# Another order for the first weights and tokens, and the adding transfers behind the first tile of the first closing

## The chip, the cores and the metric

One core of one Trainium2 chip runs the whole kernel in one launch. The metric is the device time of one execution in microseconds, as a median over runs; lower is better. A verdict compares the changed kernel with the kernel before on the same chip.

## The reference

The kernel is a two-layer decoder trunk on 512 tokens of width 1024 in float32. The first layer mixes with a gated short convolution, the second with sliding-window attention over a shared K and V; both are followed by a SwiGLU network of width 2816. Cut to the parts that the change touches:

```
def short_conv_mixer(h, w_in, conv_w, w_out):
    bcx = h @ w_in
    b_gate, c_gate, u = jnp.split(bcx, 3, axis=-1)
    y = b_gate * causal_depthwise_conv3(c_gate * u, conv_w)
    return y @ w_out

mix = short_conv_mixer(rmsnorm(h, a_pre_norm[l]), a_w_in[l], a_conv_w[l], a_w_out[l])
h = h + rmsnorm(mix, a_post_norm[l])
...
ff = swiglu(rmsnorm(h, ffn_pre_norm[l]), ffn_w_gate_up[l], ffn_w_down[l])
h = h + rmsnorm(ff, ffn_post_norm[l])
```

## The kernel before

Every float32 product is made as three faster products. A matrix is split into a high part (ScalarE rounds it, `AF.Copy` into fp32r) and a low part (VectorE subtracts the high part from the original). TensorE then adds high by high, high by low and low by high. The helper `mm3` holds these three at lines L191, L192 and L193, so nearly all products of the kernel carry one of these lines.

**The start.** The 1024 input features lie in eight token parts `xt[k]` of 128 features by 512 tokens. The first output group of the convolution needs three tiles of `w_in` (for the c, u and b gates, `first[0..2]`, 128 x 1024 each, one block of 128 columns for each `k`). For `k` from 0 to 7 there are nine products of 128 x 512 into three banks `begun[0]` (named `pcub` in the profile): three passes for each of the three tiles, 72 in all, at L687. What they read is made by `token_hi` (L675, ScalarE), `token_lo` (L678, VectorE), `first_hi` (L667, ScalarE) and `first_lo` (L671, VectorE). Ahead of them TensorE runs `WARM` products of ones by ones into an unused bank (`idle`, L663); each of them shows as two in the profile.

The inputs come by transfers that the queue of SyncE (SP) and that of ScalarE (ACT) issue. Each of the three tiles is cut by column into pieces of 256, 256 and 512 columns (`CUTS`, `piece`, L220), so that the first block of all three tiles needs three pieces. The transfers of these two queues share eight semaphores in turn, and the ninth waits until the first has landed, the tenth until the second, and so on. All instructions of TensorE, VectorE, ScalarE and GpSimd stand in the order in which they are written (`manual_schedule`), and each engine works its own list in that order.

**The adding transfers.** Some weight blocks are used as sums of blocks. The sums are made in HBM by transfers that GpSimd issues: `Sums` holds their steps (copy a block, then add another onto it), `sum_on(name)` moves all begun sums on by one step, and `issue(n)` writes the next n transfers into GpSimd's list (L535). An adding transfer waits in that list until the copy under it has landed. Such a step stands at many named places of the kernel (`BEGIN` says which sums begin where).

**The closing.** `close` multiplies the gated convolution by the second half of `w_out`, for four tiles `t` of 128 tokens and two halves of 512 columns each (`unit`, bank `pmix`, 12 products of 128 x 512 for a half), and ends the layer: `take` (L259, VectorE) adds the bank to `mix`; `square_mix` (L264, ScalarE) sums the squares; `tile_done` then scales `mix` (L290), has GpSimd take the power -1/2 of the mean (`mean`, L293 on VectorE and L297 on GpSimd), updates the residual `hs[t]` (`update`, L302, VectorE), squares it (L310), takes a second power of GpSimd for the tile before (`mean2`, L315 and L319) and writes the normalised `xn[t-1]` (`norm`, L324, ScalarE). In the last half of the last tile TensorE transposes `xn[0]` and `xn[1]` (`turn`, L335) between its products. The first closing stands at about 159 to 185 us of the profile; right ahead of it the lines

```
    with tc.manual_schedule(engines=ALL):
        sum_on("o1")
        issue(len(issues))
        close(ws, ys, 0, res, ahead)
```

put the step `o1` into GpSimd's list before any of the closing's powers: two adding transfers onto gate sums begun at `o0`, and four copies that begin the sums `d01`.

Of the kernel before, what the change touches and what calls it, by code (L numbers as in the profile page):

```python
# [10 lines left out]
F32 = mybir.dt.float32  # L11
F32R = mybir.dt.float32r
AF = mybir.ActivationFunctionType
ALU = mybir.AluOpType
PSUM = bass.MemoryType.PSUM

P = 128
D = 1024
S = 512
KT = D // P  # L20
# [18 lines left out]
)  # L39

LAST = (9, 7, 5, 3)
WARM = 10
LEAD = 2
LINE_LEAD = 3

# [27 lines left out]
def yoco_kernel(  # L73
# [139 lines left out]
    xt = [halves("xt") for _ in range(KT // 2)]  # L213
    xt = [xt[k // 2][k % 2] for k in range(KT)]
    first = [wraw.tile([P, D], F32, tag="raw", name=name("raw")) for _ in range(3)]
    CUTS = [(0, 2), (2, 4), (4, KT)]

    def piece(queue, t, c):
        c = slice(CUTS[c][0] * P, CUTS[c][1] * P)
        queue.dma_start(first[t][:, c], w_in[0, t, :, c])  # L220

    nc.scalar.dma_start(gt, gains)
    nc.sync.dma_start(xt[0], xT[0])
    piece(nc.scalar, 0, 0)
    piece(nc.sync, 2, 0)
    piece(nc.scalar, 1, 0)
    nc.sync.dma_start(xt[1], xT[1])
    for t in range(3):
        piece(nc.sync, t, 1)
    nc.sync.dma_start(xt[2], xT[2])  # L230
    nc.sync.dma_start(xt[3], xT[3])
    for t in range(3):
        piece(nc.sync, t, 2)
    for k in range(4, KT):
        nc.sync.dma_start(xt[k], xT[k])
    later = [fetch(w_in[1, t]) for t in range(min(3, N_RAW - 3))]


# [316 lines left out]
    def sum_on(at):  # L555

        issue(len(issues))
        if at in BEGIN:
            summing.append(sums_of[BEGIN[at]])
        for x in summing:  # L560
            x.step()
        summing[:] = [x for x in summing if x.steps]
# [94 lines left out]
    with tc.manual_schedule(engines=ALL):  # L657

        warm = small.tile([P, 1], F32, tag="warm", name=name("warm"))
        nc.scalar.activation(warm, ones[:, 0:1], AF.Copy)  # L660
        idle = bank("idle", ps_pt)
        for _ in range(WARM):
            nc.tensor.matmul(idle[:, :P], ones, ones, start=True, stop=True)  # L663

        def first_hi(t, k0, k1):
            c = slice(k0 * P, k1 * P)
            nc.scalar.activation(ws[t][0][:, c], first[t][:, c], AF.Copy)  # L667

        def first_lo(t, k0, k1):
            c = slice(k0 * P, k1 * P)  # L670
            nc.vector.tensor_tensor(out=ws[t][1][:, c], in0=first[t][:, c],  # L671
                                    in1=ws[t][0][:, c].bitcast(F32), op=ALU.subtract)

        def token_hi(k):
            nc.scalar.activation(xs[k][0], xt[k], AF.Copy, scale=g(G_APRE, k))  # L675

        def token_lo(k):
            nc.vector.scalar_tensor_tensor(  # L678
                out=xs[k][1], in0=xt[k], scalar=g(G_APRE, k), in1=xs[k][0].bitcast(F32),
                op0=ALU.mult, op1=ALU.subtract,  # L680
            )

        def products(k, passes):
            kk = slice(k * P, (k + 1) * P)
            for i, t in passes:
                whi, wlo = ws[t]
                nc.tensor.matmul(begun[0][t], (whi, whi, wlo)[i][:, kk],  # L687
                                 xs[k][i == 1], start=k == i == 0,
                                 stop=k == KT - 1 and i == 2)

        token_hi(0)
        for t in range(3):
            first_hi(t, 0, 1)
        first_lo(0, 0, 1)
        first_lo(1, 0, 1)
        token_lo(0)
        first_lo(2, 0, 1)
        for t in range(3):
            first_hi(t, 1, 2)
        products(0, [(0, 0), (0, 1), (0, 2), (2, 0), (2, 1), (1, 0), (1, 1), (1, 2), (2, 2)])  # L700
        for k in range(1, KT):
            token_hi(k)
            token_lo(k)
            for k0, k1 in CUTS:
                if k == max(k0 - 1, 1):
                    for t in range(3):
                        if k0:
                            first_hi(t, k0, k1)
                    for t in range(3):
                        first_lo(t, max(k0, 1), k1)  # L710
            products(k, [(i, t) for i in range(3) for t in range(3)])
        later += [fetch(w_in[1, t]) for t in range(len(later), 3)]
        for b in range(NB):
            hs[b] = wide("h")
            nc.sync.dma_start(hs[b], x[b])
        nc.sync.dma_start(mask, tables[:, 2 * S :])
        nc.sync.dma_start(snk, sinks.partition_broadcast(P))
        ws = [split_weights(None, raw, True) for raw in later[:2]]
        square(0)
        square(1)  # L720
        ws.append(split_weights(None, later[2], True))
        square(2)
# [136 lines left out]
    def tile_done(res, t, square=True):  # L859

        if t > 0:
            res.mean2(t - 1)
        res.scale(t, 0)
        res.mean(t)
        if t > 0:
            res.norm(t - 1)
        res.scale(t, 1)
        res.update(t)
        if square:
            res.square(t)  # L870

    def close(ws, x, k0, res, ahead):


        n = len(x) - k0

        def part(ps, t, half, ks):
            unit(ps, t, ws[len(ws) // 2 * half :], x, ks, n, k0)

        begun = [bank("pmix", ps_mm) for _ in range(2)]  # L880
        for half in range(2):
            part(begun[half], 0, half, range(n - 1))
            ahead.one()
            ahead.one()
        for t in range(NB):
            for half in range(2):
                if t == 0:
                    ps = begun[half]
                    part(ps, t, half, range(n - 1, n))
                else:  # L890
                    ps = bank("pmix", ps_mm)
                    if (t, half) == (NB - 1, 1):
                        part(ps, t, half, range(2))
                        for b in range(4):
                            res.turn(b, (0, 1))
                        part(ps, t, half, range(2, n))
                        for f in range(4):
                            res.split(0, f, 0)
                        res.square_mix(t, 0)
                        res.square(NB - 2)  # L900
                        res.scale(t, 0)
                    else:
                        part(ps, t, half, range(n))
                res.take(t, half, ps)
                if (t, half) != (NB - 1, 0):
                    res.square_mix(t, half)
            if t < NB - 1:
                tile_done(res, t, square=t < NB - 2)

    def last_tile(res, pieces, ahead=None):  # L910

# [42 lines left out]
    issue(len(issues))  # L954
    ahead = Ahead(first_weights(0))
    with tc.manual_schedule(engines=ALL):
        sum_on("o1")
        issue(len(issues))
        close(ws, ys, 0, res, ahead)


    def ffn(l, before, ahead, gain, gpres, following):
# [539 lines left out]
def _lay_out(x, a_pre_norm, a_w_in, a_conv_w, a_w_out, a_post_norm, ffn_pre_norm,  # L1502
# [7 lines left out]
    def stationary(w, n):  # L1510

        w = np.asarray(w)
        k = w.shape[0] // P
        return w.reshape(k, P, n, P).transpose(2, 1, 0, 3).reshape(n, P, k * P)
# [27 lines left out]
    for b in (0, HD):  # L1542
# [6 lines left out]
    tables[:, 2 * S :] = np.where((diff >= 0) & (diff < P), 0.0, -1e30)  # L1549

    wi = stationary(a_w_in[0], 3 * KT).reshape(3, KT, P, D)
    gu = np.stack([stationary(ffn_w_gate_up[l], 2 * NF).reshape(2, NF, P, D) for l in range(2)])
    gu = gu.transpose(0, 2, 1, 3, 4)
    gb = gu[:, PLAIN:].reshape(2, -1, 2, 2, P, 2, S).transpose(0, 1, 3, 5, 4, 2, 6)
# [6 lines left out]
        "behind": c(behind),  # L1561
        "sinks": c(np.asarray(b_sinks)[0][heads]),
        "tables": tables,
        "w_in": c(wi[[1, 2, 0]].transpose(1, 0, 2, 3)),
        "w_ob": c(blocks(np.asarray(a_w_out[0])[: D // 2])),
        "w_out": c(moving(np.asarray(a_w_out[0])[D // 2 :])),
        "w_gu": c(gu[:, :PLAIN]),
# [24 lines left out]
```

## Time and profile before

| | us |
|---|---|
| median of 3 runs | 1030.83 (1030.18 to 1030.97) |
| the profiled execution's own time | 1033.09 |
| its span, first to last instruction | 1031.3 |
| TensorE busy in it | 1019.1 (99%) |

The profiled execution took 2.26 us more than the median, and 1.79 us of its own time lie outside the span. In the rows of the timeline the first two numbers are the start and the duration in us; then follow the engine, the line, the operation, what is written and read, and how many are merged. The bracket at the end of a row gives the idle time of that engine ahead of it and what ended the idle time. SPq, ACTq and POOLq are the sequencers of these engines, which issue transfers; PEld is TensorE's weight load. A product's duration reaches past the start of the next, so the distance from start to start tells its cost.

### The profile page before, as it was taken

To read this page: it belongs to the slowest core of one execution; us is meant where nothing else is said; L and a number is where in the kernel's file an instruction comes from. 1 tells how busy PE (TensorE), PEld (TensorE's weight loads), DVE (VectorE), ACT (ScalarE), POOL (GpSimd) and SP (SyncE) were. 2 spreads that over 40 slices of the span, in tenths; PEclk is the share of its full clock that TensorE was granted. 3 is DMA by queue.
4 is the path that set the end of the run, shared out by engine and by line. 5 is a ranking of instruction groups with operands and counts; after the bars stand their busy time and mean duration, and the time that the engine had idled before them with its cause. 6 is when DMAs were issued, how large, how long until landed. Compare 5 with 4: busy or idle time off the path is not lost.

```text
span 1031.3 us, 17485 instructions
## 1 busy us (share of the span) xinstructions
PE 1019.1 (99%) x6650; PEld 927.5 (90%) x6650; DVE 822.4 (80%) x1404; ACT 577.6 (56%) x1039; POOL 193.9 (19%) x259
## 2 busy tenths in 40 slices
PE   9999999999999999999999999999999999999997
PEld 7888887999989899999898888889998999989986
DVE  5676666888777978878869998688886788887786
ACT  7232543865655454566466777668565554645632
POOL 0433122102101021000122663221211010200001
PEclk9999999999999999999999999999999999999999
DMA  9897789548979789868603879986889676998732
GB/s 332 288 247 232 192 251 338 167 164 253 330 237 275 262 281 301 280 209 308 194 1 128 219 206 274 256 268 164 257 283 326 184 248 201 315 299 248 246 139 82
DMA packets 66868, 244.59 MB, mean 237 GB/s; under 512 B 7904, under 2 KB 8800, under 8 KB 55008
## 3 DMA queue, kind: packets, MB, share of 16 engines
q1 hardware_dynamic: 51472, 145.91, 38.7%
q0 software_dynamic: 14592, 96.48, 36.6%
q8 instruction: 52, 0.85, 0.3%
q10 hardware_dynamic: 720, 1.08, 0.3%
q14 instruction: 32, 0.26, 0.1%
HBM read 237.15 MB, written 102.76 MB: 330 GB/s over the span
## 4 chain that ended last, share of the span: by engine, by line
PE 89%; DVE 4%; DMA 4%; ACT 1%; POOL 1%; issue 1%; ACTq 0%; DVEq 0%; POOLq 0%
PE gx L193 7%; PE gx L192 7%; PE gx L191 7%; PE gz L193 4%; PE gz L192 4%; PE gz L191 4%; PE px L191 3%; PE px L192 3%; PE px L193 3%; PE pcub L192 3%; PE pcub L193 3%; PE pcub L191 3%; DMA hsum<-in_w_gb_dram 3%; PE pmix L193 2%; PE pmix L192 2%; PE pmix L191 2%
## 5 line engine op out<-in xcount | busy, mean ns | idle before, releaser
L467 DVE TENSOR_TENSOR wlo<-raw,whi 128x1024 fp32r<-128x1024 f32 x225 | 275.1, 1227 | 94.0 <-ACT whi L466 93.9
L466 ACT ACTIVATE whi<-raw 128x1024 fp32r<-128x1024 f32 x225 | 234.3, 1050 | 120.1 <-DVE raw L454 22.0
L191 PE MATMUL gx<-xt,whi 128*128 128x256 f32 x480 | 135.8, 283 | 0.0
L192 PE MATMUL gx<-xt,whi 128*128 128x256 f32 x480 | 135.8, 283 | 0.0
L193 PE MATMUL gx<-xt,wlo 128*128 128x256 f32 x480 | 135.8, 283 | 0.0
L535 POOL DMA_DIRECT2D hsum<-in_w_gb_dram x96 | 62.9, 720 | 159.1 <-ACT whi L466 82.3
L191 PEld LDWEIGHTS gx<-xt,whi 128*128 128x128 f32 x480 | 92.2, 192 | 0.0
L192 PEld LDWEIGHTS gx<-xt,whi 128*128 128x128 f32 x480 | 92.2, 192 | 0.0
L193 PEld LDWEIGHTS gx<-xt,wlo 128*128 128x128 f32 x480 | 92.2, 192 | 0.0
L1011 ACT ACTIVATE st<-gx 128x256 f32<-128x256 f32 x80 | 30.3, 385 | 80.8 <-PE gx L193 80.8
L535 POOL DMA_DIRECT2D hsum<-hsum x32 | 25.2, 789 | 262.9 <-ACT whi L466 186.6
L192 PE MATMUL pcub<-xhi,whi 128*128 128x512 f32 x168 | 65.4, 389 | 0.0
L191 PE MATMUL pcub<-xlo,whi 128*128 128x512 f32 x168 | 65.4, 389 | 0.0
L193 PE MATMUL pcub<-xhi,wlo 128*128 128x512 f32 x168 | 65.4, 389 | 0.0
L191 PE MATMUL px<-wlo,ahi 128*128 128x512 f32 x120 | 46.7, 389 | 0.0
L193 PE MATMUL px<-whi,alo 128*128 128x512 f32 x120 | 46.7, 389 | 0.0
L192 PE MATMUL px<-whi,ahi 128*128 128x512 f32 x120 | 46.7, 389 | 0.0
L193 PE MATMUL gx<-xhi,wlo 128*128 128x256 f32 x160 | 45.3, 283 | 0.0
L191 PE MATMUL gy<-xlo,whi 128*128 128x256 f32 x160 | 45.3, 283 | 0.0
L192 PE MATMUL gy<-xhi,whi 128*128 128x256 f32 x160 | 45.3, 283 | 0.0
L193 PE MATMUL gy<-xhi,wlo 128*128 128x256 f32 x160 | 45.3, 283 | 0.0
L191 PE MATMUL gz<-xt,whi 128*128 128x256 f32 x160 | 45.3, 283 | 0.0
(268 smaller groups left out, 3120.3 us busy)
## 6 DMA issues: line engine op xcount, KB each, us to landing
hsum<-in_w_gb_dram POOLq DMA_DIRECT2D x96, 512.0 KB, 8.1
raw<-hsum SPq DMA_DIRECT2D x88, 512.0 KB, 7.8
raw<-in_w_gb_dram SPq DMA_DIRECT2D x60, 512.0 KB, 7.4
hsum<-in_w_dn_dram POOLq DMA_DIRECT2D x36, 512.0 KB, 8.3
raw<-in_w_dn_dram SPq DMA_DIRECT2D x32, 512.0 KB, 6.6
hsum<-hsum POOLq DMA_DIRECT2D x28, 512.0 KB, 5.4
raw<-in_w_in_dram SPq DMA_DIRECT2D x21, 512.0 KB, 7.8
hsum<-in_w_dn_dram POOLq DMA_DIRECT2D x12, 768.0 KB, 13.2
```

Of the source, the lines that this page charges most:

```text
L191: nc.tensor.matmul(out, whi, xlo, start=start, stop=False, **kw)
L192: nc.tensor.matmul(out, whi, xhi, start=False, stop=False, **kw)
L193: nc.tensor.matmul(out, wlo, xhi, start=False, stop=stop, **kw)
L466: self.begun = nc.scalar.activation(hi[:, :n], raw, AF.Copy)
L467: nc.vector.tensor_tensor(out=lo[:, :n], in0=raw, in1=hi[:, :n].bitcast(F32), op=ALU.subtract)
L535: nc.gpsimd.dma_start(dst, src, max_dma_last_dim=4 * 4 * S, **kw))
L1011: nc.scalar.activation(s, x, AF.Copy)
```

## The change

Three things are edited; the arithmetic of the sums stays as it was but for the order of the passes.

First, the 24 blocks (128 columns each) of the first three tiles are laid out on the host in the order in which the products use them: for `k` = 0 the blocks of the three gates, then those for `k` = 1, and so on. `first[0]` holds blocks 0 to 7, `first[1]` 8 to 15, `first[2]` 16 to 23. The pieces are now runs of this order: 384, 384 and 256 columns of the first, and halves of 512 columns of the other two. All that `k` = 0 needs of the weights is one piece, issued by SP behind `xt[0]`; the second piece is the only one on ScalarE's queue. Pieces and token parts follow each other on SP's queue in the order of use.

Second, the splitting follows the same order (the table `FIRST`), the nine products for each `k` run as high by high, low weight by high token, high weight by low token, and `WARM` is 9 instead of 10.

Third, the step `o1` of the adding transfers is handed to `close` as `then` and stands in GpSimd's list behind the first tile's power instead of ahead of it.

```
-WARM = 10
+WARM = 9
...
-    CUTS = [(0, 2), (2, 4), (4, KT)]
-    def piece(queue, t, c):
-        c = slice(CUTS[c][0] * P, CUTS[c][1] * P)
-        queue.dma_start(first[t][:, c], w_in[0, t, :, c])
+    def piece(queue, i, c0, c1):
+        queue.dma_start(first[i][:, c0:c1], w_in[0, i, :, c0:c1])
     nc.scalar.dma_start(gt, gains)
     nc.sync.dma_start(xt[0], xT[0])
-    piece(nc.scalar, 0, 0)
-    piece(nc.sync, 2, 0)
-    piece(nc.scalar, 1, 0)
+    piece(nc.sync, 0, 0, 384)
+    piece(nc.scalar, 0, 384, 768)
     nc.sync.dma_start(xt[1], xT[1])
-    for t in range(3):
-        piece(nc.sync, t, 1)
     nc.sync.dma_start(xt[2], xT[2])
+    piece(nc.sync, 0, 768, D)
+    piece(nc.sync, 1, 0, S)
     nc.sync.dma_start(xt[3], xT[3])
-    for t in range(3):
-        piece(nc.sync, t, 2)
-    for k in range(4, KT):
-        nc.sync.dma_start(xt[k], xT[k])
+    piece(nc.sync, 1, S, D)
+    nc.sync.dma_start(xt[4], xT[4])
+    piece(nc.sync, 2, 0, S)
+    nc.sync.dma_start(xt[5], xT[5])
+    piece(nc.sync, 2, S, D)
+    nc.sync.dma_start(xt[6], xT[6])
+    nc.sync.dma_start(xt[7], xT[7])
...
-        token_hi(0)
-        for t in range(3):
-            first_hi(t, 0, 1)
-        first_lo(0, 0, 1)
-        first_lo(1, 0, 1)
-        token_lo(0)
-        first_lo(2, 0, 1)
-        for t in range(3):
-            first_hi(t, 1, 2)
-        products(0, [(0, 0), (0, 1), (0, 2), (2, 0), (2, 1), (1, 0), (1, 1), (1, 2), (2, 2)])
-        for k in range(1, KT):
+        FIRST = {0: [(0, 0, P), (0, P, 384)], 1: [(0, 384, 768)], 2: [(0, 768, D), (1, 0, S)],
+                 4: [(1, S, D)], 5: [(2, 0, S)], 6: [(2, S, D)]}
+        for k in range(KT):
+            pieces = FIRST.get(k, [])
             token_hi(k)
+            for p in pieces:
+                first_hi(*p)
+            for p in pieces:
+                first_lo(*p)
             token_lo(k)
-            for k0, k1 in CUTS:
...
-            products(k, [(i, t) for i in range(3) for t in range(3)])
+            for i in range(3):
+                for t in range(3):
+                    n = 3 * k + t
+                    whi, wlo = (w[:, n % KT * P : (n % KT + 1) * P] for w in ws[n // KT])
+                    nc.tensor.matmul(begun[0][t], (whi, wlo, whi)[i], xs[k][i == 2],
+                                     start=k == i == 0, stop=k == KT - 1 and i == 2)
...
-    def close(ws, x, k0, res, ahead):
+    def close(ws, x, k0, res, ahead, then=None):
...
             if t < NB - 1:
                 tile_done(res, t, square=t < NB - 2)
+            if t == 0 and then:
+                then()
...
     with tc.manual_schedule(engines=ALL):
-        sum_on("o1")
-        issue(len(issues))
-        close(ws, ys, 0, res, ahead)
+        def sums_on():
+            sum_on("o1")
+            issue(len(issues))
+        close(ws, ys, 0, res, ahead, sums_on)
...
     wi = stationary(a_w_in[0], 3 * KT).reshape(3, KT, P, D)
+    wi = c(wi[[1, 2, 0]].transpose(1, 0, 2, 3))
+    wi[0] = wi[0].reshape(3, P, KT, P).transpose(2, 0, 1, 3).reshape(3, KT, P, P).transpose(
+        0, 2, 1, 3).reshape(3, P, D)
...
-        "w_in": c(wi[[1, 2, 0]].transpose(1, 0, 2, 3)),
+        "w_in": wi,
```

More of the change, by code (lines that the diff above doesn't have):

```diff
@@ L663, in yoco_kernel, with first_hi, first_lo @@
             nc.tensor.matmul(idle[:, :P], ones, ones, start=True, stop=True)
[L665 to L672, printed above, removed]
+        def first_hi(i, c0, c1):
+            nc.scalar.activation(ws[i][0][:, c0:c1], first[i][:, c0:c1], AF.Copy)
+        def first_lo(i, c0, c1):
+            nc.vector.tensor_tensor(out=ws[i][1][:, c0:c1], in0=first[i][:, c0:c1],
+                                    in1=ws[i][0][:, c0:c1].bitcast(F32), op=ALU.subtract)
         def token_hi(k):
@@ L681, in token_lo @@
             )
[L683 to L689, printed above, removed]
-        token_hi(0)
-        for t in range(3):
-            first_hi(t, 0, 1)
-        first_lo(0, 0, 1)
-        first_lo(1, 0, 1)
-        token_lo(0)
-        first_lo(2, 0, 1)
-        for t in range(3):
-            first_hi(t, 1, 2)
-        products(0, [(0, 0), (0, 1), (0, 2), (2, 0), (2, 1), (1, 0), (1, 1), (1, 2), (2, 2)])
-        for k in range(1, KT):
+        FIRST = {0: [(0, 0, P), (0, P, 384)], 1: [(0, 384, 768)], 2: [(0, 768, D), (1, 0, S)],
+                 4: [(1, S, D)], 5: [(2, 0, S)], 6: [(2, S, D)]}
+        for k in range(KT):
+            pieces = FIRST.get(k, [])
             token_hi(k)
+            for p in pieces:
+                first_hi(*p)
+            for p in pieces:
+                first_lo(*p)
             token_lo(k)
-            for k0, k1 in CUTS:
[L705 to L710, printed above, removed]
-            products(k, [(i, t) for i in range(3) for t in range(3)])
+            for i in range(3):
[4 more added lines that the diff above has]
+                                     start=k == i == 0, stop=k == KT - 1 and i == 2)
         later += [fetch(w_in[1, t]) for t in range(len(later), 3)]
```

## The prediction

> **What bounds the kernel now.** I read the head of the page first, then TensorE's waits, then the timeline where those waits lie.
>
> ```profile
> span 1031.3 us, 17485 instructions
> PE 1019.1 (99%) x6650; PEld 927.5 (90%) x6650; DVE 822.4 (80%) x1404; ACT 577.6 (56%) x1039; POOL 193.9 (19%) x259
> ```
>
> TensorE is busy for 99% of the span. No product is taken out, so the change can only gain where TensorE stands idle or slow, and can lose wherever it makes TensorE wait. The waits of TensorE name few such places:
>
> ```profile
> PE xt L335 <- ACT xn L324: 2.5, 1, 2.5
> PE idle L663 <- DVE ones L140: 1.1, 1, 1.1
> PE pcub L687 <- ACT whi L667: 1.0, 1, 1.0
> ```
>
> Two of the three are in the stages that the change edits: the first products (`pcub`, L687) and the transposes of the first closing (`xt`, L335). Both are waits for something upstream, so I look at each in the timeline. First TensorE at the start:
>
> ```profile
> 1.06 4.64 PE L663 MATMUL idle<-ones 128*128 128x128 f32 x20 [1.06 <-DVE ones L140]
> 5.35 0.77 PE L687 MATMUL pcub<-xhi,whi 128*128 128x512 f32 x1
> 7.13 1.22 PE L687 MATMUL pcub<-xhi,whi 128*128 128x512 f32 x2 [1.00 <-ACT whi L667]
> ...
> 9.00 1.48 PE L687 MATMUL pcub<-xlo,whi 128*128 128x512 f32 x3
> 10.28 0.56 PE L687 MATMUL pcub<-xhi,wlo 128*128 128x512 f32 x1
> 10.68 0.86 PE L687 MATMUL pcub<-xhi,whi 128*128 128x512 f32 x3
> ...
> 25.00 0.39 PE L191 MATMUL pcub<-xlo,whi 128*128 128x512 f32 x1
> ```
>
> Here the distance between starts is what to read. From 10.68 to 25.00 stand the 63 products of `k` = 1 to 7: 14.32 / 63 = 0.227 us each, with nothing missing between them. The three products from 9.00 to 10.28 take 1.28 / 3 = 0.427 us each. So the nine products of `k` = 0 cost 10.68 - 5.35 = 5.33 us, where nine at the later pace cost 2.05. Of the excess of 3.3 us, the hole between the first product and the second is 7.13 - 5.35 - 0.43 = 1.35, and the rest is the slow pace, which lasts until about 10.4, 3.3 us after the restart at 7.13. The 4.3 us of idle products ahead of 5.35 have not ended it, with that hole behind them.
>
> What filled the hole is in ScalarE's rows and in the chain of waits:
>
> ```profile
> 3.89 0.72 ACT L675 ACTIVATE xhi<-xt,gt 128x512 fp32r<-128x512 f32 x1 [0.24 <-DMA gt<-in_gains_dram]
> 4.64 0.31 ACT L667 ACTIVATE whi<-raw 128x128 fp32r<-128x128 f32 x1
> 6.76 1.11 ACT L667 ACTIVATE whi<-raw 128x128 fp32r<-128x128 f32 x5 [1.82 <-DMA raw<-in_w_in_dram]
> ...
> 10.54 0.62 ACT L667 ACTIVATE whi<-raw 128x512 fp32r<-128x512 f32 x1
> ...
> 13.14 2.74 ACT L675 ACTIVATE xhi<-xt,gt 128x512 fp32r<-128x512 f32 x4
> ```
>
> ```profile
> 1.67 5.07 DMA raw<-in_w_in_dram
> ```
>
> ScalarE had the first block at 4.64 and then stood until 6.76 for the piece of the second tile, the second transfer of weights on its own queue, issued at 1.67.
>
> Now the closing. GpSimd's rows:
>
> ```profile
> 166.31 0.80 POOL L535 DMA_DIRECT2D hsum<-in_w_gb_dram  x1 [15.19 <-DMA hsum<-in_w_gb_dram]
> 168.11 0.79 POOL L535 DMA_DIRECT2D hsum<-in_w_gb_dram  x1 [1.01 <-DMA hsum<-in_w_gb_dram]
> 168.63 2.28 POOL L535 DMA_DIRECT2D hsum<-in_w_dn_dram  x4
> 170.65 0.85 POOL L297 TENSOR_TENSOR ur<-uv,mhalf 128x1 f32<-128x1 f32 x1
> ...
> 175.92 0.92 POOL L297 TENSOR_TENSOR ur<-uv,mhalf 128x1 f32<-128x1 f32 x1 [1.03 <-DVE uv L293]
> ```
>
> VectorE's, ScalarE's and TensorE's beside them:
>
> ```profile
> 166.00 0.21 DVE L293 TENSOR_SCALAR uv<-us 128x1 f32<-128x1 f32 x1
> ...
> 171.54 1.29 DVE L302 SCALAR_TENSOR_TENSOR h<-mix,ur,h 128x1024 f32<-128x1024 f32 x1 [4.74 <-POOL ur L297]
> ```
>
> ```profile
> 180.82 1.13 ACT L324 ACTIVATE xn<-h,ur 128x1024 f32<-128x1024 f32 x1
> ```
>
> ```profile
> 179.21 0.27 PE L335 MATMUL xt<-ident,xn 128*128 128x128 f32 x1
> 182.01 1.86 PE L335 MATMUL xt<-ident,xn 128*128 128x128 f32 x15 [2.53 <-ACT xn L324]
> ```
>
> The mean of the first tile is there at 166.21, but its power starts at 170.65: GpSimd works its list in order, and ahead of the power it sat 15.19 us for a copied block to land, then waited for a second one, then issued four more. VectorE stood 4.74 us behind that power. All later tiles run late from there, `xn[1]` comes at 180.82 + 1.13 = 181.95, and TensorE's second transpose starts at 182.01 instead of about 0.11 after 179.21 (15 transposes lie in 1.6 us): 2.7 us lost.
>
> **The start, part by part.** *First product.* Its weights are now the first third of a 192 KB piece behind `xt[0]` on SP's queue. Before, a 128 KB piece was there by 4.64. The bytes ahead of it grow by 64 KB on its own queue, and by up to 64 KB on the other one, which shares the engines. The transfer rates of the first windows:
>
> ```profile
> 2.00:4.00 2.00, 2.00 (x12) 2.00 (x10) 0.00 (x0) 1.60 (x3) 0.00 (x0) 1.00 0.93 266
> 4.00:6.00 2.00, 2.00 (x9) 1.62 (x8) 0.29 (x1) 0.92 (x2) 0.00 (x0) 1.00 1.10 362
> ```
>
> The last column is GB/s, the one ahead of it the busy share of the transfer engines. At 362 GB/s, 64 KB are 0.18 us and 128 KB 0.36. So the piece lands between 4.64 and 5.0; I take 4.8. The split of 128 columns takes 0.31, so TensorE starts at about 5.15, against 5.35. One idle product less ends them 4.64 / 10 = 0.46 us earlier, at 4.9, so they are not in the way; between them and the first product stand some 0.3 us.
>
> *The hole.* The other two blocks are in the same piece, so ScalarE splits them right behind (256 columns between 0.31 and 0.62). The second product can start at 5.5, and at the slow pace it isn't due before 5.58: the hole of 1.35 goes. What is late next is the low part of the token: it starts when VectorE has made the low weights, at about 5.9, and takes some 0.7 (nearly ScalarE's 0.72 for the same tile, an estimate), to 6.6. The passes are ordered so that the six others go first, at 0.427 until 7.7. It is covered, and would cost about 0.1 if the pace were fast from the first product on.
>
> *The pace.* At 5.15 + 9 x 0.427 `k` = 0 would end at 9.0 if all its products were slow. Before, the pace changed 3.3 us after the last hole. Counted from 5.15 that is 8.45: 7.7 products slow, 1.3 fast, end at 8.75. Counted from the idle products at 1.06, which now run into the real ones almost without a hole, it could be any time up to then; if it falls at 7.0, `k` = 0 ends at 8.1. I take 8.4, against 10.68: a gain of 2.3. The bounds: pace changed before the first product, end at 5.15 + 9 x 0.227 = 7.2, or 7.5 as the splits of `k` = 0 then bind, a gain of 3.2; pace changed only at 10.4 as before, where 3.3 products of `k` = 1 run slow as well and 0.7 is lost again, a gain of 1.0. The granted clock in the windows above (third column from the right) reads 1.00 throughout, so only the distances of the products show this pace. [...]
>
> *Supply behind it.* A round of nine products takes 2.04 us. It needs 256 KB of token and 192 KB of weights, 1.27 us at 362 GB/s. ScalarE's part is 2.74 / 4 = 0.69 for a token and at most 0.62 for a piece of 512 columns; VectorE's is much the same. So `k` = 1 and later are not bound by transfers or splits. The second piece sits on ScalarE's queue, where a transfer took 5.07 us before; issued at 1.19 it would be there at 6.3, and it is needed at about 7.5. SP's later issues wait in turn for the first eight landings, as before. The removed instructions (5 on ScalarE, 4 on VectorE) are off the path.
>
> *Does the earlier start last?* TensorE then has 2.3 us less in hand against everything that runs by the transfers. Against that the list of its waits names none behind L687's until the closing.
>
> **The closing, part by part.** With the step `o1` behind it, the first power starts at 166.2, 4.4 earlier, and so does the update. The six transfers start hardly later: the first one's copy had landed shortly before 166.31 and the power ends at 167.1; the second one still waits for its landing (168.11). What waits behind them now is the second power of tile 0 (L319) and the power of tile 1 (L297). The landing is in the chain of waits:
>
> ```profile
> 150.33 17.49 DMA hsum<-in_w_gb_dram
> ```
>
> The copy issued at 150.33 lands at 167.82; the five issues from 168.11 end at 168.63 + 2.28 = 170.9. Tile 1's mean depends on TensorE: five halves of 12 products and 6 more lie ahead of 179.21, so it begins at 179.21 - 66 x 0.227 = 164.2, and its second half ends 24 products later, at 169.7. With `take` (0.65, half of VectorE's 1.29 for 1024 columns) and the square with its read-out (some 0.8, from ScalarE's 0.62 for 512 columns; both estimates) and small steps between, the mean stands at about 171.5. So GpSimd is free before it is asked. From the power of tile 1 to the second transpose were 182.01 - 175.92 = 6.1 us; from 171.6 that ends at 177.7, ahead of 179.21, where TensorE gets there by its own work. The hole of 2.7 goes, with 1.5 us to spare. The chain behind it (splits, the last tile, the feed-forward's first products) starts from those transposes and moves up with them. The bounds are 0, if the landing comes over 4 us later, and 2.7, as there is no more to gain.
>
> **The sum.** 2.3 + 2.7 = 5.0. Against the profiled execution's own 1033.09 that is 1028.1, and 1026.3 for its span. The median of the runs is 2.26 lower, so I carry the difference: 1030.83 - 5.0 = **1025.8**. About 0.2% (2.1 us) is what a measurement of this kernel can tell from no change.
>
> **The rivals.** *The timed runs had less to gain at the start* (chance 0.12). They are 2.26 us under the profiled one; part of that may be a pace that changed earlier. If it was fast from 7.13 on before, `k` = 0 ended 8 x 0.2 = 1.6 us earlier, at 9.1; against some 7.8 after, with a few of its products still slow, the start gains 1.3: 1030.83 - 1.3 - 2.7 = 1026.8.
>
> *The closing's wait only moves* (0.08). If the copies land some 4 us later, tile 1's power takes the place of tile 0's, and 2.3 remain: 1028.5. For it: the transfers are fully busy there. Against it: they are issued earlier with the rest.
>
> ```profile
> 120.00:140.00 20.00, 20.00 (x90) 16.55 (x89) 13.02 (x17) 8.13 (x11) 3.36 (x5) 1.00 0.55 163
> 140.00:160.00 20.00, 20.00 (x90) 16.57 (x89) 17.21 (x25) 8.44 (x12) 4.67 (x6) 1.00 1.02 299
> 400.00:420.00 20.00, 20.00 (x99) 16.94 (x98) 16.65 (x20) 5.32 (x5) 2.36 (x3) 1.00 1.01 319
> ```
>
> The share of 0.55 just ahead says that the transfers were not behind there, so their burst starts when GpSimd's list gets to it and moves with TensorE.
>
> *The gain is given back later* (0.07). At 400 to 420 the transfers are saturated. If they ran to a fixed time there, all but about 1 us would be lost: 1029.8, no change. Against it: the list of TensorE's waits names none of L191 to L193, which work there.
>
> *Slower* (0.04): the adding transfers hold up tile 1's power for longer than they held tile 0's. It decides from a landing 1.5 us later on (a hole opens); at 4.2 later the closing is as before; at 9 later, 2.1 us worse than the kernel before even with the start's gain. With a landing 10 us later, at 177.8: 10 - 1.5 = 8.5 of hole instead of 2.7, less 2.3: 1030.83 + 3.5 = 1034.3.
>
> *The edit does nothing at the start* (0.04): the 192 KB piece lands at 6.7 like the piece that was late before, the first product starts at 7.1 behind a hole, and `k` = 0 ends as late as before: 1030.83 - 2.7 = 1028.1.
>
> **How the numbers follow.** My forecast has 0.65. Of it and the rivals, faster by over 0.2% (under 1028.8) are the forecast, the first, most of the second, and the last: 0.87. Within 0.2%: the gain given back and the rest of the moved wait, 0.08. Slower: 0.05, with 0.01 for what I have not seen. The range goes from 3.2 + 2.7 = 5.9 and about a microsecond of spread between executions, 1024.0, to the moved wait, 1028.6.
>
> **What would show it.** Right: the first L687 at about 5.1, no gap to the second, `k` = 1 starting between 7.2 and 9.0, L191 at 22.0 to 24.0 instead of 25.00; the power L297 directly behind its mean, ahead of the six L535; no wait `xt` on `xn` in TensorE's list; a span of 1026 or so. Wrong: an idle time of ScalarE's L666 ahead of `k` = 0 or 1, a slow pace past 10, a wait of VectorE's L302 for the second L297, or a new wait of TensorE between 185 and 500.

## The result

The changed kernel took 1027.93 us in the median of 21 runs (1027.09 to 1032.91), the kernel before on the same chip 1031.89 us (21 runs, 1029.23 to 1036.92). The ratio is 0.9969, with an interval of 0.9958 to 0.998: faster by 3.2 us, between 2.1 and 4.3. The medians lie 3.96 us apart, the means 3.2. The forecast was faster by 5.0. The three runs behind the 1030.83 from which it was counted are the first three of these 21, whose median is 1031.89.

The profiled execution of the changed kernel is not one of the usual ones: its own time is 1032.36 us, 4.43 over the median, and only 0.73 under the 1033.09 of the profiled execution before. Here is the head of its page, and TensorE's waits with what ended them:

```profile
span 1030.6 us, 17465 instructions
...
PE 1019.1 (99%) x6648; PEld 927.8 (90%) x6648; DVE 823.2 (80%) x1400; ACT 577.7 (56%) x1035; POOL 195.3 (19%) x259
```

```profile
PE xt L335 <- ACT xn L324: 2.7, 1, 2.7
PE idle L663 <- DVE ones L140: 1.1, 1, 1.1
```

The wait of `pcub` on the split weights is gone from this list. A wait of the transposes `xt` on `xn` still stands there, once, with 2.7 us. By name and size it looks like the wait that the edit was to remove. It is another one. The timeline shows TensorE at the start and at the first closing:

```profile
1.06 4.21 PE L663 MATMUL idle<-ones 128*128 128x128 f32 x18 [1.06 <-DVE ones L140]
5.26 1.65 PE L695 MATMUL pcub<-xhi,whi 128*128 128x512 f32 x3
6.71 0.91 PE L695 MATMUL pcub<-xhi,wlo 128*128 128x512 f32 x3
7.45 0.86 PE L695 MATMUL pcub<-xlo,whi 128*128 128x512 f32 x3
8.14 0.85 PE L695 MATMUL pcub<-xhi,whi 128*128 128x512 f32 x3
...
22.43 0.39 PE L191 MATMUL pcub<-xlo,whi 128*128 128x512 f32 x1
...
176.62 1.91 PE L335 MATMUL xt<-ident,xn 128*128 128x128 f32 x16
```

There is no bracket behind the first product, so nothing idles there. The first three products cost (6.71 - 5.26) / 3 = 0.48 us each, the next three 0.25, and from 8.14 to 22.43 it is 14.29 / 63 = 0.227 again. `k` = 1 starts at 8.14 instead of 10.68. At the first closing the sixteen transposes are one group of 1.91 us without a bracket: the hole of 2.7 is gone. GpSimd's rows show why:

```profile
163.70 0.95 POOL L297 TENSOR_TENSOR ur<-uv,mhalf 128x1 f32<-128x1 f32 x1 [16.46 <-DVE uv L293]
164.61 1.66 POOL L535 DMA_DIRECT2D hsum<-in_w_gb_dram  x2
165.72 2.57 POOL L535 DMA_DIRECT2D hsum<-in_w_dn_dram  x4
168.13 0.99 POOL L319 TENSOR_TENSOR ur<-uv,mhalf 128x1 f32<-128x1 f32 x1
169.12 0.92 POOL L297 TENSOR_TENSOR ur<-uv,mhalf 128x1 f32<-128x1 f32 x1
```

The first power waits for its own mean now, and the six transfers behind it wait for no landing. Together the two edits bring every product from 185 us on forward by 5.36 us, as far as 682 us. There it ends, in the second closing, which the change does not touch. TensorE's rows of the changed kernel there:

```profile
681.95 0.27 PE L335 MATMUL xt<-ident,xn 128*128 128x128 f32 x1
684.90 2.39 PE L335 MATMUL xt<-ident,xn 128*128 128x128 f32 x15 [2.69 <-ACT xn L324]
686.94 0.77 PE L191 MATMUL pmix<-wlo,ohi 128*128 128x512 f32 x1
...
687.94 0.63 PE L193 MATMUL pmix<-whi,olo 128*128 128x512 f32 x1
688.37 0.63 PE L191 MATMUL pmix<-wlo,ohi 128*128 128x512 f32 x1
688.80 0.63 PE L192 MATMUL pmix<-whi,ohi 128*128 128x512 f32 x1
```

and the same place in the kernel before:

```profile
687.30 1.91 PE L335 MATMUL xt<-ident,xn 128*128 128x128 f32 x16
```

The second transpose comes 2.95 us after the first instead of 0.11. Behind that hole the products stand 0.43 us apart (688.37 to 688.80) and not 0.227. The windows give the granted clock, as a share of TensorE's full clock, beside it (third column from the right):

```profile
676.00:682.00 6.00, 6.00 (x28) 4.84 (x27) 4.82 (x9) 4.32 (x8) 1.48 (x2) 1.00 1.00 251
682.00:685.00 3.00, 0.32 (x3) 0.10 (x2) 1.92 (x5) 2.79 (x7) 1.42 (x2) 1.00 0.94 376
685.00:690.00 5.00, 5.00 (x25) 4.47 (x26) 4.27 (x8) 3.62 (x8) 0.06 (x1) 0.66 0.31 125
```

So of 5.36 us the hole takes 2.84 and the half clock another 1.65, and 0.87 are left; the own times of the two profiled executions differ by 0.73. What filled the hole is in GpSimd's list of the changed kernel:

```profile
671.22 0.80 POOL L535 DMA_DIRECT2D hsum<-in_w_dn_dram  x1 [9.00 <-DMA hsum<-in_w_dn_dram]
673.02 0.79 POOL L535 DMA_DIRECT2D hsum<-in_w_dn_dram  x1 [1.00 <-DMA hsum<-in_w_dn_dram]
673.56 0.85 POOL L297 TENSOR_TENSOR ur<-uv,mhalf 128x1 f32<-128x1 f32 x1
```

and of the kernel before:

```profile
675.44 0.79 POOL L535 DMA_DIRECT2D hsum<-in_w_dn_dram  x1 [0.60 <-DMA hsum<-in_w_dn_dram]
675.98 0.85 POOL L297 TENSOR_TENSOR ur<-uv,mhalf 128x1 f32<-128x1 f32 x1
```

It is the pattern of the first closing once more: two adding transfers ahead of the first power, each waiting for a landing. TensorE came 5.36 us earlier, the landing and so the power only 675.98 - 673.56 = 2.42. In the kernel before, the normalised tile is done just in time:

```profile
686.14 1.14 ACT L324 ACTIVATE xn<-h,ur 128x1024 f32<-128x1024 f32 x1
```

It ends at 687.28, and the second transpose was due at 687.41. There were 0.13 us to spare, which no list of waits shows.

### The profile page after: what moved, and what is told of

The parts are those of the page before. It is cut to its first block, busy times and chain, and to the rows that moved or that the text cites. A ratio compares the mean times of both kernels' runs of the same rounds, so it can differ in the third digit from the quotient of the medians.

```text
span 1030.6 us, 17465 instructions
## 1 busy us (share of the span) xinstructions
PE 1019.1 (99%) x6648; PEld 927.8 (90%) x6648; DVE 823.2 (80%) x1400; ACT 577.7 (56%) x1035; POOL 195.3 (19%) x259
## 4 chain that ended last, share of the span: by engine, by line
PE 90%; DVE 4%; DMA 3%; ACT 1%; issue 1%; POOL 1%; DVEq 0%; ACTq 0%
PE gx L193 7%; PE gx L192 7%; PE gx L191 7%; PE gz L193 4%; PE gz L192 4%; PE gz L191 4%; PE pcub L192 4%; PE pcub L193 4%; PE pcub L191 4%; PE px L191 4%; PE px L192 4%; PE px L193 4%; PE pmix L192 2%; PE pmix L191 2%; PE pmix L193 2%; DMA hsum<-in_w_gb_dram 2%
## 5 line engine op out<-in xcount | busy, mean ns | idle before, releaser
L191 PE MATMUL gx<-xt,whi 128*128 128x256 f32 x480 | 135.8, 283 | 0.0
L191 PEld LDWEIGHTS gx<-xt,whi 128*128 128x128 f32 x480 | 92.2, 192 | 0.0
L191 PE MATMUL pcub<-xlo,whi 128*128 128x512 f32 x168 | 65.4, 389 | 0.0
L191 PE MATMUL px<-wlo,ahi 128*128 128x512 f32 x120 | 46.7, 389 | 0.0
L191 PE MATMUL gy<-xlo,whi 128*128 128x256 f32 x160 | 45.3, 283 | 0.0
L191 PE MATMUL gz<-xt,whi 128*128 128x256 f32 x160 | 45.3, 283 | 0.0
```

Of the source, the lines that this page charges most:

```text
L191: nc.tensor.matmul(out, whi, xlo, start=start, stop=False, **kw)
```

## The experiments

The profile left a riddle: its two executions differ by 0.73 us, the runs by 3.2 (by the ratio), and the prediction said 5.0. Theory A: both parts of the change pay their 2.3 and 2.7 us in every execution, and the difference from 5.0 goes at the second closing. Theory B: the profiled execution of before, 2.26 us over the median of the first three runs, was one of the worse ones just in these two places, so that usual executions had less to gain; the second closing costs only some executions.

**The parts alone, and the second closing as well.** `start_only` is the changed kernel with the first closing as before:

```
-    def close(ws, x, k0, res, ahead, then=None):
+    def close(ws, x, k0, res, ahead):
...
-            if t == 0 and then:
-                then()
...
-        def sums_on():
-            sum_on("o1")
-            issue(len(issues))
-        close(ws, ys, 0, res, ahead, sums_on)
+        sum_on("o1")
+        issue(len(issues))
+        close(ws, ys, 0, res, ahead)
```

> The changed start (layout of the first weights, order of the transfers, 9 idle products), with the adding transfers ahead of the first closing as in the kernel before. In the trace k = 1 should start near 8.1 us and L191 near 22.5, as in the changed kernel, and the hole at the first closing should still be there. Theory A (each part pays in full where it stands, and the second closing takes some back): 2.6 us at the start; the first closing's hole grows where the landings do not move up with TensorE, and a hole opens in the second closing, where the kernel before had none to spare; in sum 1.0 to 2.0 us faster. Theory B (the timed executions of the kernel before had less to gain at the start, since their slow pace ended earlier): 1.0 to 1.5 us faster, with no hole at the second closing.

`closing_only` is the opposite: the kernel before with the step `o1` behind the first tile.

```
-    def close(ws, x, k0, res, ahead):
+    def close(ws, x, k0, res, ahead, then=None):
...
+            if t == 0 and then:
+                then()
...
-        sum_on("o1")
-        issue(len(issues))
-        close(ws, ys, 0, res, ahead)
+        def sums_on():
+            sum_on("o1")
+            issue(len(issues))
+        close(ws, ys, 0, res, ahead, sums_on)
```

> The start as in the kernel before, and only the step o1 of the adding transfers moved behind the first tile of the first closing. The first closing's hole of 2.7 us should be gone. Theory A: 2.7 us there, less up to 2.5 us where a hole opens at the second closing; in sum 1 to 2.5 us faster. Theory B: 2.7 us faster, all of it kept.

`second_too` is the changed kernel with the last two adding transfers of the second closing behind its first tile too:

```
-                if op in "RH":
+                if op in "RH" and i < KT + 1:
                     issue(len(issues) // 2 if op == "R" else len(issues))
-            sum_on(f"a{i + 1}")
+            if i < KT + 1:
+                sum_on(f"a{i + 1}")
...
-        close(rest_w, at, EARLY, res, ahead)
+        close(rest_w, at, EARLY, res, ahead, lambda: sum_on(f"a{KT + 2}"))
```

> The changed kernel, and in the second closing also the last two adding transfers behind the first tile's power instead of ahead of it. Theory A: the hole of 2.85 us before the second closing's transposes and the slow products behind it (another 1.7 us) are gone in every execution, so the spread upwards (4 of 21 runs 3 to 5 us over the rest) disappears, and the median is 4.5 to 5.5 us under the kernel before. Theory B: the spread disappears too, but the median stays within 0.5 us of the changed kernel's, as most of its executions have no such hole.

`after_again` is the changed kernel, unedited, on the chip of the other three.

> The changed kernel once more, on the same chip as the three others. Theory A and B: 3.2 us faster than the kernel before, with single runs 3 to 5 us over the others. Its profile tells whether the hole at the second closing is there in another execution: A says at least in part (over 0.5 us), B says not in a run of the lower group.

On this chip the kernel before took 1030.92 us (median of 31 runs):

| | median (range), runs | ratio to before |
|---|---|---|
| `start_only` | 1029.91 (1028.76 to 1031.32), 12 | 0.999 [0.9982, 0.9999] |
| `closing_only` | 1029.05 (1028.02 to 1034.73), 12 | 0.9984 [0.997, 0.9998] |
| `after_again` | 1028.29 (1027.19 to 1032.08), 12 | 0.998 [0.9969, 0.9991] |
| `second_too` | 1027.39 (1027.18 to 1028.09), 8 | 0.9966 [0.9954, 0.9977] |

By medians the start alone brings 1.0 us, the closing alone 1.9, both 2.6. So the parts about add up, and neither is worth what the profiled execution showed. These times do not part the theories: the 1.0 of `start_only` stands at the lower end of both expectations, and the 1.9 of `closing_only` lies in A's 1 to 2.5 and short of B's 2.7, with an interval of 0.2 to 3.1 that holds both. The profiles speak against A. It let the first hole of `start_only` grow and a hole open at the second closing; the first hole is 1.55 us there instead of 2.69, and neither `start_only` nor `closing_only` has one at the second closing. Both profiled executions are among the fastest of their twelve, though. `second_too` fits neither: A had 4.5 to 5.5 us against the kernel before, B at most 0.5 against the changed kernel, and by medians it was 3.5 and 0.9. What A says of the second closing holds in some executions. The profiled execution of `after_again`, 1032.08 us, has the same loss:

```profile
681.14 0.27 PE L335 MATMUL xt<-ident,xn 128*128 128x128 f32 x1
683.75 2.72 PE L335 MATMUL xt<-ident,xn 128*128 128x128 f32 x15 [2.33 <-ACT xn L324]
```

And in `second_too` GpSimd's list at this closing reads:

```profile
670.58 0.94 POOL L297 TENSOR_TENSOR ur<-uv,mhalf 128x1 f32<-128x1 f32 x1 [9.12 <-DVE uv L293]
671.48 1.66 POOL L535 DMA_DIRECT2D hsum<-in_w_dn_dram  x2
```

The power waits for its own mean, the two transfers behind it for nothing, and TensorE has no wait on `xn` at all.

**Three more executions of the kernel before.** `before_look1`, `before_look2` and `before_look3` are the kernel before without an edit, for the profile of each.

> The kernel before, unchanged, in another profiled execution. Theory B (the first profile was an execution with both losses near their largest; the usual one has less to gain): k = 1 starts anywhere from 8.7 to 10.7 us, by when the full pace begins, and the hole of the first closing lies anywhere from 0 to 2.7; the own time is 1033.1 less what these two lack of 10.68 and 2.7, within 0.5 us. Theory A (both losses are the same in every execution, the difference arises at the second closing): k = 1 at 10.7 and a hole of 2.7 again, and an own time under 1032 with neither of them smaller.

> The same once more: theory B expects another start of k = 1 between 8.7 and 10.7 and another hole between 0 and 2.7, theory A 10.7 and 2.7.

> The same once more: theory B expects another start of k = 1 between 8.7 and 10.7 and another hole between 0 and 2.7, theory A 10.7 and 2.7.

TensorE at the start of `before_look1` (1030.8 us) and of `before_look2` (1033.59 us):

```profile
4.94 0.50 PE L687 MATMUL pcub<-xhi,whi 128*128 128x512 f32 x1
6.77 0.74 PE L687 MATMUL pcub<-xhi,whi 128*128 128x512 f32 x2 [1.32 <-ACT whi L667]
...
8.80 0.85 PE L687 MATMUL pcub<-xhi,whi 128*128 128x512 f32 x3
```

```profile
4.96 0.47 PE L687 MATMUL pcub<-xhi,whi 128*128 128x512 f32 x1
7.08 0.74 PE L687 MATMUL pcub<-xhi,whi 128*128 128x512 f32 x2 [1.65 <-ACT whi L667]
...
9.12 0.85 PE L687 MATMUL pcub<-xhi,whi 128*128 128x512 f32 x3
```

The hole is there, as long as in the first profile or longer (in `before_look3` it is shorter, 0.54 us idle). But the eight products behind it take 8.80 - 6.77 = 2.03 us and 9.12 - 7.08 = 2.04, where they took 10.68 - 7.13 = 3.55 in the execution that the prediction read. The pace was fast before the hole ended. The hole of the first closing differs as well. In the first profile the power started at 170.65, 8.56 us ahead of the first transpose at 179.21. In `before_look1` the first transpose is at 177.30, and GpSimd's rows are:

```profile
163.18 0.80 POOL L535 DMA_DIRECT2D hsum<-in_w_gb_dram  x1 [15.01 <-DMA hsum<-in_w_gb_dram]
165.26 0.79 POOL L535 DMA_DIRECT2D hsum<-in_w_gb_dram  x1 [1.28 <-DMA hsum<-in_w_gb_dram]
...
167.81 0.86 POOL L297 TENSOR_TENSOR ur<-uv,mhalf 128x1 f32<-128x1 f32 x1
```

The power starts 9.49 us ahead of it, so 0.93 earlier in this measure, and the hole is 1.75 us instead of 2.69. This speaks for theory B, and against A, which expected 10.7 and 2.7 again in each of the three: none has `k` = 1 later than 9.12, and `before_look3` has 8.68 with a hole of 1.88. And `before_look2` shows holes at both closings, so the second one is not the change's own:

```profile
PE xt L335 <- ACT xn L324: 4.3, 2, 2.4
```

**A longer run of idle products.** `before_warm14` is the kernel before with more products ahead of the first, to have the pace fast in time.

```
-WARM = 10
+WARM = 14
```

> The kernel before with 14 idle products instead of 10, so that TensorE works on until about 7.0 us, where the late piece of weights is split, and no hole lies among the first products; the transfers are as before. [...] If the pace depends on the real products alone, it changes at 10.4 again and the time stays within 0.3 us, or is worse where idle products push the first one back.

1030.01 us (1028.88 to 1030.82, 11 runs) against 1030.66 (15 runs), ratio 0.9993 [0.9984, 1.0002]: no difference that can be told. The gain of half a microsecond or more, the author's estimate, was not shown. The trace says why: the 14 idle products run until 6.24, so the first product starts 0.9 to 1.3 us later than in the three executions above, a hole of 0.91 us is left behind it, and the eight after the hole take 9.64 - 7.63 = 2.01, as in those three. In usual executions there was no slow pace to cure.

**The last comparison**, on one chip with the kernel before at 1030.44 us (20 runs). `both_closings` has the start of before and both closings with the transfers behind the first tile (the edits of `closing_only` and `second_too`); `second_again` is `second_too` and `after_third` the changed kernel, both without an edit.

> The start as in the kernel before; in the first and in the second closing the adding transfers stand behind the first tile's power. What is left against the next kernel is the start alone, with no closing that could hide or return it. If the start is worth what the first profile showed (10.68 to some 8.1), this kernel is 2.3 to 2.6 us slower than the next one; if it is worth what the other looks showed (8.7 to 9.1 against 7.3 to 8.3), 1.0 to 1.4 us slower. Against the kernel before it loses the closing's hole of 1.8 to 2.7 us and the second closing's of 0 to 2.1: 2 to 3 us faster. No hole in either closing.

> The changed kernel with the second closing's last two adding transfers moved as well, once more beside the other two. 3.3 to 4.0 us faster than the kernel before, all runs within about 1.2 us of each other, 0.3 to 1 us under the changed kernel in the median and more in the mean.

> The changed kernel beside the other two: 2.6 to 3.5 us faster than the kernel before, with one or two of a dozen runs 3 to 5 us over the others. In its profile the hole at the second closing is either under 0.5 us with an own time under 1029, or over 2 us with a half clock of 3.4 us behind it and an own time over 1031.

| | median (range), runs | ratio to before |
|---|---|---|
| `both_closings` | 1028.18 (1027.79 to 1028.44), 10 | 0.9976 [0.9967, 0.9985] |
| `second_again` | 1027.68 (1027.14 to 1029.06), 7 | 0.9974 [0.9963, 0.9985] |
| `after_third` | 1027.68 (1027.27 to 1029.59), 9 | 0.9972 [0.9962, 0.9982] |

Between `both_closings` and `second_again` lies only the start: 0.5 us by these medians, where 1.0 to 1.4 or more were expected, and 0.8 against `second_too` on the other chip. `second_again` is 2.8 us under the kernel before, short of the expected 3.3 to 4.0, and not under the changed kernel. `after_third` is an execution of the changed kernel whose second closing has no hole. GpSimd's rows there:

```profile
667.70 0.80 POOL L535 DMA_DIRECT2D hsum<-in_w_dn_dram  x1 [7.42 <-DMA hsum<-in_w_dn_dram]
669.40 0.79 POOL L535 DMA_DIRECT2D hsum<-in_w_dn_dram  x1 [0.90 <-DMA hsum<-in_w_dn_dram]
669.94 0.85 POOL L297 TENSOR_TENSOR ur<-uv,mhalf 128x1 f32<-128x1 f32 x1
```

The order is that of the execution with the hole, but the waits are 7.42 and 0.90 us instead of 9.00 and 1.00, and the power starts at 669.94 instead of 673.56. Whether the changed kernel loses there depends on when these copies land. Why they land earlier in one execution than in another was not followed up.

**All profiles side by side.** For each, the start of `k` = 1, the hole at each closing (the largest distance between two transposes, less 0.11), and the loss to the half clock behind it. The sum is what these differ by from the first profile of before; beside it stands what the own times differ by.

| profile | own us | `k` = 1 | first hole | second hole, half clock | sum | measured |
|---|---|---|---|---|---|---|
| before | 1033.09 | 10.68 | 2.69 | 0 | | |
| `before_look1` | 1030.80 | 8.80 | 1.75 | 0.24 | 2.6 | 2.3 |
| `before_look2` | 1033.59 | 9.12 | 2.53 | 2.09 | -0.4 | -0.5 |
| `before_look3` | 1031.11 | 8.68 | 1.88 | 0.92 | 1.9 | 2.0 |
| `before_warm14` | 1030.82 | 9.64 | 1.13 | 0.34 | 2.3 | 2.3 |
| `closing_only` | 1028.37 | 8.78 | 0 | 0 | 4.6 | 4.7 |
| `both_closings` | 1028.23 | 8.65 | 0 | 0 | 4.7 | 4.9 |
| `start_only` | 1028.76 | 7.37 | 1.55 | 0 | 4.5 | 4.3 |
| after | 1032.36 | 8.14 | 0 | 2.84, 1.65 | 0.7 | 0.7 |
| `after_again` | 1032.08 | 7.29 | 0 | 2.50, 1.68 | 1.9 | 1.0 |
| `after_third` | 1027.27 | 7.48 | 0 | 0 | 5.9 | 5.8 |
| `second_too` | 1028.09 | 8.30 | 0 | 0 | 5.1 | 5.0 |
| `second_again` | 1027.14 | 7.37 | 0 | 0 | 6.0 | 6.0 |

Three places account for every profiled execution to within 0.3 us, but for `after_again`, which lost some 0.8 more between 918 and 928 us (not followed up). The start of before, unedited, gives `k` = 1 at 8.65 to 9.12 in five executions and at 10.68 only in the first. The mean of the five is 8.8; that of the six executions with the new start is 7.7. So the start's usual gain is about 1.1 us (1.5 if the 10.68 is counted in), and the first closing's hole is 1.13 to 2.53 in the five other profiles that have that order, in the mean 1.8. That is 2.9 together. Measured were 3.2 by the ratio in the first comparison, and 2.6 and 2.8 by medians in the two later ones.

**Does `second_too` beat the changed kernel?** On one chip its median is 0.9 us lower, on the other the two are equal, and the intervals overlap: not shown in the median. Of the changed kernel's 42 runs in three comparisons five were above 1031 us, the two profiled ones with the hole among them; of the 15 of `second_too` none was above 1029.06, and of the 10 of `both_closings` none above 1028.44. That fits a loss that strikes some executions and is taken away, but 15 runs without one would be no rarity either (0.88 to the fifteenth is 0.15).

## Why the prediction came out as it did

*First product and hole.* Right. The first product was forecast at 5.15 and came at 5.26 (4.94 to 5.24 in the five others of this start); no hole behind it; the low parts came in time.

*Pace.* Near, and in part by luck: `k` = 0 was to end at 8.4 instead of 10.68 and ended at 8.14, with L191 at 22.43 in the range of 22.0 to 24.0. But 10.68 and 8.14 are one execution each, and the other profiles of these two starts have 8.65 to 9.12 and 7.29 to 8.30. The granted clock of 1.00 that the prediction read at 2 to 6 us was no reading: the profile has no record of this clock before the first full grant, at 10.63 us in that execution, and a window without a record shows 1.00. The lower bound of 7.5, where the splits were to bind, was too high: four of the six executions have `k` = 1 at 7.29 to 7.48.

*Supply.* Right: 63 products at 0.227, no wait. ScalarE lost four instructions and not five (x1039 to x1035), which changes nothing.

*First closing.* Right. The power was to start at 166.2 less the start's gain, so at 163.7 with the gain of 2.5, and did so at 163.70; tile 1's power was forecast at 171.6, less the same gain 169.1, and came at 169.12. Only the second transfer's landing was taken too late: the two issues have no wait between them. The hole of 2.7 went.

*The sum and its carrying over.* Here the prediction failed. The two gains were 2.54 and 2.7 in the profiled execution, 5.36 as TensorE's rows have it, against 5.0. But the step "the median of the runs is 2.26 lower, so I carry the difference" takes it that the 2.26 us lay somewhere else. They lay for the most part in the two losses themselves. `before_look1`, close to the median on its chip, shows where: `k` = 1 is 1.88 earlier and the hole 0.94 shorter. A usual execution had about 2.9 of these 5.0 to give. The rival "the timed runs had less to gain at the start" was the nearest to what happened, and its 1.3 us for the start fits the 1.1. It got 0.12, and it kept the closing at the full 2.7, where the mean of the other executions is 1.8. The time of 1025.8 was missed by 2.1 us, and 1.1 of these come from elsewhere: the median of the kernel before was 1031.89 in the 21 runs and not 1030.83.

*What stayed behind it.* The prediction asked whether the earlier start lasts and took the list of waits for an answer: "none behind L687's until the closing". It held up to 682. A list of waits shows what is late already. It does not show what is 0.13 us from being late, and the same list had been read for the first closing only, though the kernel has a second one with the same order. This is the rival "the closing's wait only moves" in a place that it did not name, and it strikes some executions. By the medians it is small: where the second closing was mended, the median was 0.9 us lower on one chip and the same on the other. The sign that the prediction gave for a loss, a new wait of TensorE between 185 and 500, lay short of it. In the rival "slower", which did not come, the landing 9 us later should read 2.5 us worse by its own terms (7.5 - 2.7 - 2.3), not 2.1.

## What to carry to other kernels

The losses that one reads in a profiled execution slower than the median may be the very reason that it is slower; look for each loss in several executions before summing, or take the smaller end for the median. A wait that one edit removes is worth looking for at every place where the code has the same order, here a small operation queued behind a transfer that waits for a landing. And before a large step forward is booked, measure the slack of the next places that are fed by transfers: what ends 0.13 us in time now is late once the rest moves up by 5.

## What had not been expected of the hardware

The pace of the first products is a matter of the execution. With the same instructions ahead of them, the eight products behind the hole took 3.55 us once and 2.02 to 2.04 in the five other profiles of that start; with the new start the nine took 2.24 to 2.35 in four executions and 2.88 and 3.13 in two. So the 10.68 was one draw, and the prediction took it for the usual value. The clock records of the first profiles have the first full clock at 10.63 us (before) and at 6.81 (the changed kernel).

These two records tell more. In both the changes of the granted clock lie whole multiples of 3.4133 us apart: in before 298 of them, 1017.17 us, from the full clock at 10.63 to the half clock at 1027.80; in the changed kernel 199, 679.25 us, from the full clock at 6.81 to the half clock at 686.06, then one, to the full clock at 689.48, and 99, 337.92 us, to the half clock at 1027.40. So each of the two executions can be cut into stretches of this length. In before TensorE idled 0.67 us in the stretch from 0.39 to 3.80, as it starts at 1.06, and 1.00 us in the next, which holds the hole; the third, to 10.63, had no idle time, and the full clock came at its end. In the changed kernel TensorE idled 1.06 us in the stretch that ends at 3.40 and not at all in the next, and the full clock came at the end of this one, at 6.81. The hole alone does not make the pace late: `before_look1` and `before_look2` have it too, and the eight products behind it took 2.03 and 2.04 us there. With the new start no hole follows the first product. That the hole's place among the stretches made the pace late is the author's estimate from these two traces; no run was made to test it.

The clock behind a hole varies as well. After holes of TensorE of 2.69 and 2.33 us (after, `after_again`, second closing) products stood 0.43 us apart for a while and 1.65 and 1.68 us were lost. After holes of 2.53 (before, first closing) and 2.37 us (`before_look2`, first closing) they did not:

```profile
177.68 0.27 PE L335 MATMUL xt<-ident,xn 128*128 128x128 f32 x1
180.32 1.86 PE L335 MATMUL xt<-ident,xn 128*128 128x128 f32 x15 [2.37 <-ACT xn L324]
181.93 0.47 PE L191 MATMUL pmix<-wlo,yhi 128*128 128x512 f32 x1
182.24 0.39 PE L192 MATMUL pmix<-whi,yhi 128*128 128x512 f32 x1
```

Here the fifteen transposes take 1.61 us, and in the changed kernel's second closing 2.04. The length of the hole alone doesn't decide it: behind 2.33 us the clock fell, behind 2.53 it did not. Its place among the stretches of 3.4133 us fits. TensorE's busy time is the first number behind the comma; two stretches of the changed kernel at the second closing, then the stretch of the kernel before that holds most of its first hole:

```profile
682.65:686.06 3.41, 1.16 (x11) 1.16 (x12) 2.47 (x4) 2.74 (x7) 1.40 (x2) 1.00 0.69 278
686.06:689.48 3.42, 3.42 (x13) 2.93 (x12) 3.09 (x7) 2.93 (x7) 0.00 (x0) 0.50 0.41 165
```

```profile
177.88:181.29 3.41, 1.59 (x8) 1.04 (x6) 2.67 (x7) 2.97 (x7) 0.59 (x2) 1.00 1.02 424
```

In the first of them TensorE idles 2.25 us, and the next one runs at half clock, 3.41 us long. In the kernel before the hole of 2.53 is shared by two stretches, 1.82 and 0.71 us, and the clock stayed at 1.00. So in these two profiles the full clock was kept behind the stretch with 1.82 us of idle time and withdrawn behind the one with 2.25; no run was made to test this either.
